# Layer 0 of a two-layer recurrence step in a new order: weight look-ahead, first merges, query products, first key copies

## The chip, the cores and the metric

The kernel runs on one core of a Trainium2 chip. The metric is the time of one execution on the device, in microseconds (us). Three runs of the kernel before gave 788.27, 791.18 and 792.0 us (median 791.18); the execution that was profiled took 789.21 us, of which 787.4 us are the span of the trace.

The engines have short names in the profile: PE is TensorE (matmuls; PEld its weight loads), DVE is VectorE, ACT is ScalarE, POOL is GpSimd, SP is SyncE, which here only issues DMAs. ACT issues DMAs as well. Each engine runs its own instructions strictly in the order in which they stand, and waits at an instruction until the semaphores that it names have come.

## What is computed

One inference step of a two-layer backbone on 128 context tokens and 512 latent tokens (640 tokens, five tiles of 128), width 1024. Layer 0 has two groups of heads, HGRN2 (4 heads, keys of 128) and GLA (4 heads, keys of 64); layer 1 is a retention layer and is not touched here. Each layer is

```python
h = rms_norm(x) * (1 + scale) + shift        # shift, scale, gate = SiLU(cond) @ ada_w + ada_b
p = h @ w_in                                 # queries, keys, values, gates, forget gates
S_t = diag(g_t) S_{t-1} + k_t v_t^T          # one scan per direction, per head
o_t = S_t^T q_t                              # both directions are added
out = (group_rms_norm(o) * silu(gate)) @ w_out
x = x + gate * out
```

In layer 0 the decay g_t differs for every key channel, so that a score between two tokens carries the product of all decays between them.

## The kernel before, in words

Every projection is done in three matmuls, (high, high), (high, low) and (low, high), on operands that were split into a rounded part and a remainder. Weights come in 168 blocks of 128x512: SP loads `raw` (L171, five buffers), ACT rounds it into `wh` (L180), DVE makes the remainder `wl` (L182); `weights(i, look)` issues blocks up to `look` ahead of the one that is used. The activations of layer 0 are split in the same way into `h0h` (ACT, L489) and `h0l` (DVE, L490).

The first stage, from about 20 to 60 us, is the projection `pbv` of the GLA values, in eight steps k. Beside step k the modulation of the activations for step k + 1 is finished (`padv`, `ab`, `xnt`, then `h0h` and `h0l`), and the modulation sums `pada` for step k + 2 run on PE.

Then layer 0 goes through six rows: two GLA rows (two heads each) and four HGRN rows (one head each). A row first projects its queries, keys or forget gates (`pf`, evacuated into `q`, `K` and the decays `T`, which the code calls `g1`). HGRN rows compute K and T from the gates (L817, L819), and `ks`, the sum of both directions' keys (L821). `prepare` multiplies the queries by the decays, once for each direction, into `Q` (L654, L655). The generator `row` then does the scores `px` in a pyramid of seven levels h = 1 ... 64: level h takes a copy `km` of keys in pairs of blocks (`kmix`, ACT, L685), 20 or 40 small matmuls per head on PE, and a masked copy into `A` (L712); then `merge(h)` multiplies half of K (L693) and half of Q (L695) by the decays of their block, and multiplies decays of neighbouring blocks into the table of the next level (L697). After the seventh level K is transposed on PE (`pkt`), copied to `kt` by ACT (L723), multiplied with the values (`pkv`, on PE), and the chunk states `S` are updated on DVE (`states`, L403 and L406: six updates). The outputs are `po<-v,A` and then `po<-S,Q`.

The order on PE is written out by hand: `run` issues the projection of the next row and, whenever a model clock says so, one step of a row (`add_bg`, `step`). The order on the other engines is made by a scheduler, which places an instruction by its priority (as a rule the place at which it was issued) and by when it believes that its inputs are ready. So the steps of two successive rows mix: the projection of row h + 1 runs on PE between the levels of row h, and K, T, ks, Q, the first `km` and the first merge of row h + 1 are issued close to where row h has its `kt`, its states and its outputs.

Of the kernel before, what the change touches and what calls it, by code (L numbers as in the profile page):

```python
# [17 lines left out]
T = 640  # L18
KC = 8
# [9 lines left out]
LOOK = 5  # L29
# [12 lines left out]
def hybrid_kernel(  # L42
# [357 lines left out]
    def states(kv, s, decay, st, out):  # L400

        for n in range(3):
            V.scalar_tensor_tensor(s[:, 0, n + 1, :], s[:, 0, n, :], decay(0, n + 1),  # L403
                                   kv[0][:, 128 * (n + 1):128 * (n + 2)], op0=MUL, op1=ADD)
            m = 3 - n
            V.scalar_tensor_tensor(s[:, 1, m - 1, :], s[:, 1, m, :], decay(1, m + 1),  # L406
                                   kv[1][:, 128 * m:128 * (m + 1)], op0=MUL, op1=ADD)
        for d in range(2):
            S.copy(st[:, d, :], kv[d][:, 0:128])
        ACTQ.dma_start(out, st)  # L410

    def kv_products(heads, kt, vcol):
# [127 lines left out]
    for k in range(KC):  # L540
        wh, wl = weights(ids_bv[k], 1 if k < 6 else LOOK)
        if k + 3 < KC:
            chunks[k + 3] = ada_first(k + 3)
        if k == 5:
            gkw = tokt("gkw")[:, 0:512].rearrange("p (d n) -> p d n", d=2)
            G.memset(gkw, 0.0)
            for gg in range(4):
                for d in range(2):
                    ACTQ.dma_start(gkw[32 * gg + 16 * d:32 * gg + 16 * d + 16, d, :], gla_gk_w[0, d])
            wbl = tokt("wbl")[:, 0:256].rearrange("p (k n) -> p k n", k=KC)  # L550
            ACTQ.dma_start(wbl, w0.rearrange("(k p) n -> p k n", p=128)[:, :, C_BL:C_BL + 32])
        for t in range(NT):
            g, o = group_of(t)
            three(pv[t], wh[:, 0, :], wl[:, 0, :], act[g][0][:, k, o:o + 128], act[g][1][:, k, o:o + 128],
                  k == 0, k == KC - 1, swap=True)
            if k + 1 < KC and t == 0:
                for _ in fin:
                    pass
                first_h(k + 1, 0)
                first_h(k + 1, 1)  # L560
            if k + 2 < KC and t == 1:
                fin = ada_first_mm(k + 2, chunks[k + 2])
                next(fin)
# [86 lines left out]


    def prepare(Q, q, g1):

        G.tensor_tensor(Q[:, 0, :], q, g1[:, 0, :], op=MUL)  # L654
        G.tensor_tensor(Q[:, 1, :], q, g1[:, 1, :], op=MUL)  # L655

    def row(q, g1, K, Q, diag, heads, vcol, ycol, s0, out, y_t, gn):
# [41 lines left out]

        km = kmix(1)  # L700
        kmat, dscale = diag
# [3 lines left out]
        for n, h in enumerate(LEVELS):  # L705
            xs = scores(km, qmix(h))
            merge(h)
            if h < 64:
# [10 lines left out]
        for d, tiles in enumerate((FWD_TILES, BWD_TILES)):  # L719
            p = ps("pkt")  # L720
            for i, t in enumerate(tiles):
                transpose(p[:, 128 * i:128 * i + 128], K[:, d, 128 * t:128 * t + 128])
            S.copy(kt[:, d], p.rearrange("p (t n) -> p t n", t=4))  # L723
        yield D_KT
        kv = kv_products(heads, kt, vcol)
        st = rows.tile([128, 2, 128], F32, tag="st", name="st")
        t128 = g[0]
        states(kv, s, lambda d, t: t128[:, d, t:t + 1], st, out)
        yield D_KV
# [42 lines left out]
    for r in range(2):  # L772
        K, Q, q, g1 = gla[r]

        def use_bq(g, p, q=q):
            off, n = GROUPS[g]
            S.activation(q[:, off:off + n], p[:, :n], AF.Copy, scale=0.125)

        def use_bk(g, p, K=K):
            off, n = GROUPS[g]  # L780
            V.tensor_copy(K[:, 0, off:off + n], p[:, :n])
            S.copy(K[:, 1, off:off + n], p[:, :n])

# [13 lines left out]
    for h in range(4):  # L797
# [22 lines left out]
        ks = t25("ks")  # L820
        G.tensor_tensor(ks, K[:, 0, :], K[:, 1, :], op=ADD)  # L821
        prepare(Q, q, g1)
# [243 lines left out]
```

## Time and profile before

| | |
|---|---|
| median of three runs | 791.18 us |
| the profiled execution | 789.21 us, its span 787.4 us |
| TensorE | 751.2 us busy, 95% of the span |
| VectorE, ScalarE, GpSimd busy | 456.5, 334.7, 90.5 us |
| granted clock, mean over the span | 0.996 of full speed |

The time of a busy TensorE can't be shortened by an order of other engines; what an order can change is the time in which TensorE stands still, and the time in which its clock is low. In a timeline row the bracket at the end tells how long the engine stood still before the instruction, and which instruction of which engine it waited for last. A merged row (x20) stands for a run of like instructions, and its duration for all of them together.

### The profile page before, as it was taken

The numbers are of one execution on the slowest core, as the hardware profiler recorded it, in microseconds if no ns is written. First come the engines' busy times: TensorE is split into PE (matmuls) and PEld (weight loads), VectorE is DVE, ScalarE is ACT, GpSimd is POOL, SyncE is SP. The second block draws the span as 40 slices with busy tenths as digits, with TensorE's granted clock in tenths as the row PEclk, the third lists the DMA queues.
The fourth block names the chain that finished last, engine by engine and source line by source line (L and its number), as shares of the span: only waits on it lengthen the run. The fifth ranks groups of instructions, "written<-read, shape, count | busy, mean of one in ns | idle before, by whom it ended". The sixth has DMA issues, their size and how long they took to land.

```text
span 787.4 us, 15421 instructions
## 1 busy us (share of the span) xinstructions
PE 751.2 (95%) x6116; PEld 658.6 (84%) x6116; DVE 456.5 (58%) x886; ACT 334.7 (43%) x757; POOL 90.5 (11%) x121
## 2 busy tenths in 40 slices
PE   4989889999989999999999999999999999999996
PEld 3668878799989898788888888999999998888885
DVE  4874993844886858563557650346454546336543
ACT  6448734444635353343436450433332432335322
POOL 2000301012130314000001000001121111000101
PEclk9999999999999999999999999999999999999999
DMA  8983440464333331238235520434333332534003
GB/s 286 336 255 111 154 132 25 139 205 125 111 124 119 109 109 50 47 107 261 94 108 174 201 83 25 137 103 102 95 80 113 86 111 81 190 111 133 29 13 134
DMA packets 104775, 98.61 MB, mean 125 GB/s; under 512 B 7660, under 2 KB 80896, under 8 KB 104704
## 3 DMA queue, kind: packets, MB, share of 16 engines
q1 hardware_dynamic: 83520, 82.15, 33.5%
q10 hardware_dynamic: 21184, 15.49, 7.4%
q8 instruction: 48, 0.79, 0.4%
q14 instruction: 23, 0.19, 0.1%
HBM read 86.31 MB, written 8.16 MB: 120 GB/s over the span
## 4 chain that ended last, share of the span: by engine, by line
PE 81%; DVE 10%; issue 4%; DMA 2%; ACT 2%; POOL 1%; ACTq 0%; POOLq 0%; DVEq 0%; SPq 0%
PE pt L85 34%; PE pf L85 24%; PE po L85 6%; PE px L85 5%; PE pkv L85 3%; PE pbv L85 3%; PE pada L85 2%; DVE K L693 2%; DVE wl L182 1%; PE pyt L89 1%; DMA raw<-in_w_in_even_dram 1%; PE pkt L89 1%; DVE Q L695 1%; DVE T L697 1%; DVE A L712 1%
## 5 line engine op out<-in xcount | busy, mean ns | idle before, releaser
L182 DVE TENSOR_TENSOR wl<-raw,wh 128x512 fp32r<-128x512 f32 x168 | 115.5, 704 | 103.1 <-ACT wh L180 98.5
L180 ACT CAST wh<-raw 128x512 fp32r<-128x512 f32 x168 | 103.0, 621 | 90.3 <-PE pf L85 43.0
L85 PE MATMUL pf<-h0h,wh 128*128 128x384 f32 (+1 forms) x256 | 63.2, 328 | 0.0
L85 PE MATMUL pf<-h1h,wh 128*128 128x384 f32 (+1 forms) x256 | 60.3, 317 | 0.0
L85 PE MATMUL pf<-h0l,wh 128*128 128x384 f32 (+1 forms) x256 | 58.4, 309 | 0.0
L85 PE MATMUL pf<-h1l,wh 128*128 128x384 f32 (+1 forms) x256 | 58.3, 309 | 0.0
L85 PE MATMUL pf<-h1h,wl 128*128 128x384 f32 (+1 forms) x256 | 58.3, 309 | 0.0
L85 PE MATMUL pf<-h0h,wl 128*128 128x384 f32 (+1 forms) x256 | 58.3, 309 | 0.0
L685 ACT COPY km<-K 128x640 f32<-128x640 f32 x42 | 32.8, 782 | 52.3 <-DVE K L693 36.7
L333 DVE SCALAR_TENSOR_TENSOR y<-po,rr,gn 128x128 f32<-128x128 f32 x80 | 24.4, 346 | 52.8 <-POOL rr L158 52.8
L85 PE MATMUL pt<-wh,h1h 128*128 128x512 f32 x160 | 53.9, 402 | 0.0
L85 PE MATMUL pt<-wh,h1l 128*128 128x512 f32 x160 | 52.1, 390 | 0.0
L85 PE MATMUL pt<-wl,h1h 128*128 128x512 f32 x160 | 52.0, 390 | 0.0
L156 POOL TENSOR_SCALAR rv<-ss 128x3 f32<-128x3 f32 (+1 forms) x32 | 9.6, 300 | 350.5 <-ACT junk L325 350.0
L695 DVE TENSOR_TENSOR Q<-Q,T 128x640 f32<-128x640 f32 x42 | 38.1, 908 | 14.7 <-PE px L85 14.6
L325 ACT ACTIVATE junk<-po 128x128 f32<-128x128 f32 x80 | 22.3, 279 | 51.8 <-PE po L85 33.8
L693 DVE TENSOR_TENSOR K<-K,T 128x640 f32<-128x640 f32 x42 | 39.8, 948 | 7.2 <-ACT km L685 5.3
L85 PE MATMUL pt<-wh,h0h 128*128 128x512 f32 x120 | 43.5, 428 | 0.0
L85 PEld LDWEIGHTS pf<-h0h,wh 128*128 128x128 f32 x256 | 39.0, 189 | 4.6 <-issue 2.2
L85 PEld LDWEIGHTS px<-Q,km 64*64 64x64 f32 (+1 forms) x1120 | 29.5, 136 | 14.4 <-issue 8.6
L85 PE MATMUL px<-Q,km 64*64 64x64 f32 (+1 forms) x1120 | 35.2, 229 | 4.7 <-DVE Q L695 3.6
L85 PE MATMUL pt<-wh,h0l 128*128 128x512 f32 x120 | 39.7, 396 | 0.0
(218 smaller groups left out, 1594.8 us busy)
## 6 DMA issues: line engine op xcount, KB each, us to landing
raw<-in_w_in_even_dram SPq DMA_DIRECT2D x64, 256.0 KB, 2.9
araw<-in_ada_w_dram SPq DMA_DIRECT2D x64, 256.0 KB, 4.3
raw<-in_w_in_odd_dram SPq DMA_DIRECT2D x64, 256.0 KB, 3.0
ada<-in_ada_w_dram SPq DMA_DIRECT2D x16, 512.0 KB, 5.8
raw<-in_w_out_even_dram SPq DMA_DIRECT2D x24, 256.0 KB, 3.0
rot<-qk ACTq DMA_DIRECT2D x32, 128.0 KB, 3.4
raw<-in_w_out_odd_dram SPq DMA_DIRECT2D x16, 256.0 KB, 3.0
x<-xr SPq DMA_DIRECT2D x5, 512.0 KB, 2.8
```

The lines of the kernel that those rows point to most:

```text
L85: PE.matmul(out, lhsT, rhs, **kw)
L89: PE.transpose(out, in_, ident[0:in_.shape[0], 0:in_.shape[0]])
L156: G.tensor_scalar(v[:, :n], ssum, 1.0 / count, EPS, op0=MUL, op1=ADD)
L180: S.copy(wh, raw)
L182: V.tensor_tensor(wl, raw, wh.bitcast(F32), op=SUB)
L325: S.activation(junk, p[:, 128 * i:128 * i + 128], AF.Square, accum_out=ss[:, j:j + 1])
L333: V.scalar_tensor_tensor(dst, p[:, 128 * i:128 * i + 128], r[:, j:j + 1], dst if have else gn[:, col:col + 128], op0=MUL, op1=MUL)
L685: S.copy(km.rearrange("p (n b h) -> p n b h", b=2, h=h), ap(kf, 0, ([2 * h, T // (2 * h)], [T + h, 2], [1, h])))
L693: V.tensor_tensor(keys, keys, ap(th, 1, ([nn - 1, 2], [2, nb], [0, h])), op=MUL)
L695: V.tensor_tensor(queries, queries, ap(th, 0, ([nn + 1, 2], [2, nb], [0, h])), op=MUL)
L697: V.tensor_tensor(t2, ap(th, 0, ([nn, 2], [2, nb])), ap(th, 1, ([nn, 2], [2, nb])), op=MUL)
L712: V.copy_predicated(A[:, :, 0:64], mask[:, n, :].unsqueeze(1).to_broadcast([128, NT, 64]), x)
```

## The change

Five edits, all in layer 0. The instructions of PE and their order stay the same, row for row.

1. Look-ahead: in the first stage the blocks beyond the next are issued at step k = 7 instead of k = 6. Beside it the small gate weights `gkw` are loaded by two DMAs and spread to the other 96 partitions by three copies on POOL, where eight DMAs on ACT's queue loaded every part.
2. `behind("kt")`: the first `km` of a row is issued behind the `kt` copies of the row before it.
3. `behind("state")`: the first merge of a row (all three multiplications) is issued behind the last state update of the row before it.
4. `prepare` is one multiplication over 1280 columns on DVE instead of two over 640 on POOL, and `ks` moves from POOL to DVE.
5. The copies out of `pf` into `q` and `K` of the GLA rows are issued with high priority.

```diff
@@ states @@
-            V.scalar_tensor_tensor(s[:, 1, m - 1, :], s[:, 1, m, :], decay(1, m + 1),
-                                   kv[1][:, 128 * m:128 * (m + 1)], op0=MUL, op1=ADD)
+            end = V.scalar_tensor_tensor(s[:, 1, m - 1, :], s[:, 1, m, :], decay(1, m + 1),
+                                         kv[1][:, 128 * m:128 * (m + 1)], op0=MUL, op1=ADD)
...
+        return end
@@ first stage @@
-        wh, wl = weights(ids_bv[k], 1 if k < 6 else LOOK)
+        wh, wl = weights(ids_bv[k], 1 if k < KC - 1 else LOOK)
...
-            for gg in range(4):
-                for d in range(2):
-                    ACTQ.dma_start(gkw[32 * gg + 16 * d:32 * gg + 16 * d + 16, d, :], gla_gk_w[0, d])
+            for d in range(2):
+                ACTQ.dma_start(gkw[16 * d:16 * d + 16, d, :], gla_gk_w[0, d])
+            for gg in range(1, 4):
+                G.tensor_copy(gkw[32 * gg:32 * gg + 32], gkw[0:32])
@@ rows @@
+    last = {}
+    def behind(what):
+        return tc.issue_after(last[what].ins) if what in last else ExitStack()
...
-        G.tensor_tensor(Q[:, 0, :], q, g1[:, 0, :], op=MUL)
-        G.tensor_tensor(Q[:, 1, :], q, g1[:, 1, :], op=MUL)
+        V.tensor_tensor(Q, q.unsqueeze(1).to_broadcast([128, 2, T]), g1, op=MUL)
...
-        km = kmix(1)
+        with behind("kt"):
+            km = kmix(1)
...
-            merge(h)
+            with behind("state" if h == 1 else None):
+                merge(h)
...
-            S.copy(kt[:, d], p.rearrange("p (t n) -> p t n", t=4))
+            last["kt"] = S.copy(kt[:, d], p.rearrange("p (t n) -> p t n", t=4))
...
-        states(kv, s, lambda d, t: t128[:, d, t:t + 1], st, out)
+        last["state"] = states(kv, s, lambda d, t: t128[:, d, t:t + 1], st, out)
...
-            S.activation(q[:, off:off + n], p[:, :n], AF.Copy, scale=0.125)
+            with tc.high_priority():
+                S.activation(q[:, off:off + n], p[:, :n], AF.Copy, scale=0.125)
...
-            V.tensor_copy(K[:, 0, off:off + n], p[:, :n])
-            S.copy(K[:, 1, off:off + n], p[:, :n])
+            with tc.high_priority():
+                V.tensor_copy(K[:, 0, off:off + n], p[:, :n])
+                S.copy(K[:, 1, off:off + n], p[:, :n])
...
-        G.tensor_tensor(ks, K[:, 0, :], K[:, 1, :], op=ADD)
+        V.tensor_tensor(ks, K[:, 0, :], K[:, 1, :], op=ADD)
```

Three places show what the scheduler makes of it. The first is ACT in the first stage, from the `h0h` casts of step 5 to those of step 7 (`arow` copies the sums of a modulation step). Before:

```order
L257 COPY arow<-pada 128x128
L180 CAST wh<-raw 128x512
L549 DMA gkw<-in_gla_gk_w_dram 16x256 x3
L180 CAST wh<-raw 128x512 x3
L489 CAST h0h_111<-xnt_109 128x256
L489 CAST h0h_113<-xnt_109 128x384
L257 COPY arow<-pada 128x128
L180 CAST wh<-raw 128x512 x4
L489 CAST h0h_111<-xnt_109 128x256
L489 CAST h0h_113<-xnt_109 128x384
L180 CAST wh<-raw 128x512 x2
```

Now:

```order
L257 COPY arow<-pada 128x128
L180 CAST wh<-raw 128x512 x5
L257 COPY arow<-pada 128x128
L180 CAST wh<-raw 128x512
L490 CAST h0h_111<-xnt_109 128x256
L490 CAST h0h_113<-xnt_109 128x384
L180 CAST wh<-raw 128x512 x2
L490 CAST h0h_111<-xnt_109 128x256
L490 CAST h0h_113<-xnt_109 128x384
L180 CAST wh<-raw 128x512 x2
```

The casts of step 7 (the last two `h0h`) have two weight casts ahead of them where they had four, those of step 6 have six where they had four; the `arow` of step 7 stands behind five of these six.

The second is ACT between the second and the third HGRN row. Before:

```order
L685 COPY km<-K 128x640
L715 COPY A<-px 64x5x64
L716 COPY A<-px 64x5x64
L685 COPY km<-K 128x640
L180 CAST wh<-raw 128x512
L723 COPY kt<-pkt 128x512 x2
L409 COPY st<-pkv 128x128 x2
L410 DMA out_dram<-st 128x2x128
```

Now:

```order
L724 COPY A<-px 64x5x64
L725 COPY A<-px 64x5x64
L180 CAST wh<-raw 128x512
L732 COPY kt<-pkt 128x512 x2
L692 COPY km<-K 128x640
L409 COPY st<-pkv 128x128 x2
L410 DMA out_dram<-st 128x2x128
L692 COPY km<-K 128x640
```

Both `km` copies of the next row stood ahead of the old row's `kt`; now both stand behind it, the second one also behind the copies `st` of the states.

The third is DVE at the same kind of boundary, between the first two HGRN rows (T with a number is a decay table; K, T_25xx belong to the next row, Q with 5x64 and S to the old one). Before:

```order
L817 TENSOR_SCALAR K<-T_2528,nclb,clb 128x1280
L819 TENSOR_SCALAR T_2528<-T_2528,clb,lbv 128x1280
L695 TENSOR_TENSOR Q<-Q,T_2805 128x2x5x64
L693 TENSOR_TENSOR K<-K,T_2528 128x2x320
L697 TENSOR_TENSOR T_3061<-T_2528 128x640
L693 TENSOR_TENSOR K<-K,T_3061 128x2x160x2
L697 TENSOR_TENSOR T_3113<-T_3061 128x320
L182 TENSOR_TENSOR wl<-raw,wh 128x512
...
L403 SCALAR_TENSOR_TENSOR S<-S,T_2878,pkv 128x128 x3
```

Now:

```order
L828 TENSOR_SCALAR K<-T_2522,nclb,clb 128x1280
L830 TENSOR_SCALAR T_2522<-T_2522,clb,lbv 128x1280
L832 TENSOR_TENSOR ks<-K 128x640
L662 TENSOR_TENSOR Q<-q,T_2522 128x1280
L702 TENSOR_TENSOR Q<-Q,T_2799 128x2x5x64
L182 TENSOR_TENSOR wl<-raw,wh 128x512
L403 SCALAR_TENSOR_TENSOR S<-S,T_2871,pkv 128x128 x3
L406 SCALAR_TENSOR_TENSOR S<-S,T_2871,pkv 128x128 x3
L700 TENSOR_TENSOR K<-K,T_2522 128x2x320
L704 TENSOR_TENSOR T_3054<-T_2522 128x640
L704 TENSOR_TENSOR T_3106<-T_3054 128x320
L700 TENSOR_TENSOR K<-K,T_3054 128x2x160x2
```

The first two merges of the next row's keys and its decay tables moved from ahead of the state updates S to behind them; `ks` and the product into Q are new on DVE and stand ahead of the old row's last query merge.

## Rows read from the trace of the kernel before

**Rows 1.** The page, part 1: busy us of each engine, share of the span, instructions

```profile
PE 751.2 (95%) x6116; PEld 658.6 (84%) x6116; DVE 456.5 (58%) x886; ACT 334.7 (43%) x757; POOL 90.5 (11%) x121
```

**Rows 2.** The timeline of PE: start, us, line, tile, count [idle before <-releaser]

```profile
56.31 0.50 PE L85 MATMUL pbv<-wh,h0h 128*128 128x512 f32 x1 [2.07 <-ACT h0h L489]
...
92.73 0.46 PE L85 MATMUL px<-q,K 64*64 64x64 f32 x16 [1.22 <-DVE K L781]
...
94.18 1.05 PE L85 MATMUL px<-Q,km 64*64 64x64 f32 x40 [0.99 <-ACT km L685]
...
100.46 0.83 PE L85 MATMUL px<-Q,km 64*64 64x64 f32 x40 [2.27 <-DVE Q L695]
...
104.43 0.81 PE L85 MATMUL px<-Q,km 64*64 64x64 f32 x40 [0.30 <-DVE Q L695]
...
226.22 1.03 PE L89 MATMUL pkt<-ident,K 128*128 128x128 f32 x8
...
230.38 2.05 PE L85 MATMUL pkv<-v,kt 128*128 128x128 f32 x16 [2.23 <-ACT kt L723]
...
235.03 1.50 PE L85 MATMUL po<-S,Q 128*128 128x128 f32 x12
...
270.02 2.05 PE L85 MATMUL pkv<-v,kt 128*128 128x128 f32 x16 [1.79 <-ACT kt L723]
...
314.31 0.49 PE L85 MATMUL po<-S,Q 128*128 128x128 f32 x2 [0.78 <-DVE S L403]
...
316.33 1.40 PE L85 MATMUL po<-S,Q 128*128 128x128 f32 x10 [1.53 <-DVE S L406]
```

**Rows 3.** The timeline of ACT, 53 to 57 us

```profile
54.47 0.62 ACT L180 CAST wh<-raw 128x512 fp32r<-128x512 f32 x1 [2.39 <-DMA raw<-in_w_in_even_dram]
...
55.85 0.81 ACT L489 CAST h0h<-xnt 128x256 fp32r<-128x256 f32 x2
```

**Rows 4.** The timeline of DVE, first GLA row, 81 to 100 us

```profile
81.27 1.49 DVE L757 TENSOR_TENSOR T<-T,Q 128x1280 f32<-128x1280 f32 x1
...
84.14 4.04 DVE L182 TENSOR_TENSOR wl<-raw,wh 128x512 fp32r<-128x512 f32 x2
...
95.44 0.68 DVE L182 TENSOR_TENSOR wl<-raw,wh 128x512 fp32r<-128x512 f32 x1
...
96.04 2.18 DVE L693 TENSOR_TENSOR K<-K,T 128x640 f32<-128x640 f32 x1
...
98.55 1.77 DVE L695 TENSOR_TENSOR Q<-Q,T 128x640 f32<-128x640 f32 x1
```

**Rows 5.** The timeline of ACT, first GLA row

```profile
80.89 0.74 ACT L777 ACTIVATE q<-pf 128x384 f32<-128x384 f32 x2
```

**Rows 6.** The timeline of ACT between the first two HGRN rows

```profile
228.41 0.79 ACT L685 COPY km<-K 128x640 f32<-128x640 f32 x1 [3.41 <-DVE K L693]
...
229.74 1.07 ACT L723 COPY kt<-pkt 128x512 f32<-128x512 f32 x2
```

**Rows 7.** The timeline of DVE between the first two HGRN rows

```profile
222.23 0.95 DVE L817 TENSOR_SCALAR K<-T,nclb,clb 128x1280 f32<-128x1280 f32 x1
...
226.20 2.17 DVE L693 TENSOR_TENSOR K<-K,T 128x640 f32<-128x640 f32 x1
...
230.56 0.83 DVE L693 TENSOR_TENSOR K<-K,T 128x640 f32<-128x640 f32 x1
...
233.27 1.11 DVE L403 SCALAR_TENSOR_TENSOR S<-S,T,pkv 128x128 f32<-128x128 f32 x3
```

**Rows 8.** The timeline of POOL, two places

```profile
24.60 0.52 POOL L546 MEMSET gkw<- 128x512 f32 x1 [7.85 <-PE pada L85]
...
225.56 2.13 POOL L654 TENSOR_TENSOR Q<-q,T 128x640 f32<-128x640 f32 x1
```

**Rows 9.** The timeline of DVE between the last two HGRN rows

```profile
309.78 3.33 DVE L697 TENSOR_TENSOR T<-T 128x320 f32<-128x320 f32 x2
```

**Rows 10.** Stretches: PE, PEld, DVE, ACT, POOL busy, granted clock, DMA share, GB/s

```profile
317.00:321.00 4.00, 4.00 (x18) 3.42 (x17) 0.81 (x3) 1.12 (x7) 1.05 (x2) 0.57 0.32 76
```

## The prediction

> **What bounds the kernel now.** I read the page's first part, then the waits of TensorE, then around each long wait the timelines of the engine that ended it. TensorE is busy 751.2 of 787.4 us [rows 1], and the order of its instructions does not change, so a gain can come only from its idle time and from its clock. The reader is to see in its timeline that layer 0 has a dozen waits [rows 2], and that they are of four kinds: one in the first stage (2.07), a cluster in the first GLA row (1.22, 0.99, 2.27 and three short ones, the longest 0.30), one at `pkv` behind each of the first two HGRN rows (2.23, 1.79), and a pair at the last one (0.78, 1.53). One more of 0.71 in the second GLA row stays, because the rows around it stand as before. [...]
>
> **First stage (edit 1).** TensorE waits at 56.31 for the `h0h` cast of step 7, which starts at 55.85; the weight casts ahead of it in ACT's order wait for their raw blocks, the one at 54.47 for 2.39 us [rows 2, 3]. The block whose load ends this wait now stands elsewhere: two casts are ahead of step 7, of blocks that are loaded earlier. The two casts and the remainder on VectorE leave perhaps 0.3 us of the 2.07. In exchange step 6 has six weight casts ahead of it, and the last needs a buffer that VectorE frees only after the remainder of the block five places earlier. Nothing in the trace times this load in its new place: if it lands as late as the one in rows 3, the old wait reappears one step earlier and the edit wins nothing; if it lands when it is wanted, nothing is lost. I take 0.2 us, nearer to the second, since ACT no longer issues six of eight `gkw` DMAs between its casts. Edit 1 gives 2.07 - 0.3 - 0.2, about 1.6 us.
>
> The three new copies on GpSimd lie beside VectorE's work of the same steps. Each costs between 0.52 (the memset of 128x512, write only) and 2.13 us (a product with two inputs, 128x640) [rows 8], three 1.6 to 6.4; I take 2, near the memset, because a copy has one input. Their reader stands behind the whole stage, so on the path they cost nothing themselves. But while GpSimd works, an update of K takes 2.17 us on VectorE, without it 0.83 [rows 7]; if the copies do to the remainders and `h0l` what GpSimd's products do to K, VectorE gets 0.83/2.17 of its work done beside them. At 2 us of copies it falls back by 1.2 us, in a stage where it was not last; at 6.4 us by 4, and then all of the 1.6 is gone. [...]
>
> **First GLA row (edits 4 and 5).** The copy of K that TensorE awaits at 92.73 stands in VectorE's order behind the gates of the second row; with priority it comes ahead of them, and the first `km` with it: 1.22 + 0.99 = 2.2 us go. What is late next is the second level. It needs the first merge of Q, which ends VectorE's unbroken queue. In that queue, before, GpSimd's products stretched two remainders to 4.04 where one alone takes 0.68, K to 2.18 and Q to 1.77 where 0.83 is normal [rows 4, 7]: 2.7 + 1.35 + 0.94 = 5.0 us that go. Added are two products over 1280 columns, at the 1.49 of the nearest row (two inputs, same columns) [rows 4], 3.0 us, since the one of the second row is ahead of the merge too; the copies of q, which now come in ACT ahead of half of the logarithms, 0.74 [rows 5]; and some 0.5 of waiting for ACT, less one masked copy of 0.5. VectorE arrives 5.0 - 3.0 - 0.74 = 1.3 us earlier, and the second level starts near 99.2 instead of 100.46 [rows 2]. So of the 2.2 only 1.3 stay: the wait of 2.27 grows to about 3.2. Behind it the decay tables of the second row have left the queue; I count 0.4 of the three short waits. Together 1.7 us. The product is bounded by 1.49 from a row without collision and by 2 x 2.13, what GpSimd took; at the far end the second level is 5.5 us later, and the row loses 4.
>
> **HGRN rows (edits 2, 3 and 4).** Here the mechanism is plain in ACT. `pkt` is done at 227.2 [rows 2]; `kt` is copied at 229.74 only, because `km` of the next row stands ahead and waits 3.41 us for the merge of K on VectorE, itself slow beside GpSimd [rows 6, 7]. Now `kt` stands behind one weight cast that was issued already. It starts at 227.2, takes 1.07, and TensorE, which has projection work until 228.15, finds it ready: at most 0.1 us of each wait is left, 2.1 + 1.7 = 3.8 us gone. The postponed `km` and merge have time: the next row's levels come on TensorE only behind the outputs, which start at 235.03 [rows 2].
>
> What is late next is `po<-S,Q`, for it needs the six state updates. Before, they began at 233.27 behind the next row's merge and tables [rows 7]. Now VectorE's order from 222.23 is K and T (2 x 0.95), `ks` (0.83), the product (1.49), the last merge of Q (0.83) and one remainder (0.68): free at 228. The products `pkv` run from 228.2 for 2.05 us; the updates follow them half way through, 2 x 1.11, and end near 231.5. TensorE wants them, by its distance in rows 2 (235.03 - 232.43 = 2.6 us after `pkv`), at 232.8. That leaves 1.3 us of slack. At the last boundary, VectorE's tables were stretched to 3.33 us [rows 9] in front of the updates; tables and merges now stand behind them, and GpSimd is silent. Of 0.78 + 1.53 I leave 0.2: 2.1 us. Without the pair the clock has no reason to fall there: 1.7 us more.
>
> **Sum.** 1.6 + 1.7 + 3.8 + 2.1 + 1.7 = 10.9 us. Against the profiled execution's own 789.21 that is 778.3. The median of the runs lies 2.0 higher; the mean of all four executions is 790.2, and from that the forecast is 779.3 us.
>
> **Rivals.** (a) The clock falls in the first GLA row. The idle time of some 3.2 us before the second level is longer than any of rows 2, none of which but the last pair brought the clock down. If it falls there as it did behind that pair, 1.7 us are lost again: 781.0. For it: the pair together was only 2.3 us. Against it: 2.27 us at this very place brought nothing down. [...]
>
> (b) The first stage gains nothing, because the wait moves to step 6 or the copies on GpSimd hold VectorE up: 779.3 + 1.6 = 780.9, and with a further 1 us at step 7, 782.
>
> (c) The change doesn't do what it says at the HGRN rows: the weight cast that stands ahead of `kt` waits for its block or for a free buffer as long as `km` did, and the outputs wait for the states. Then only 1.6 + 1.7 remain of the sum, with some of the last pair: 786. Against it: between the end of `km` at 229.20 and `kt` at 229.74 [rows 6] there was room for the cast alone, so it waited for nothing.
>
> (d) Slower than before. VectorE keeps its 2.17 us per 640 columns with GpSimd silent (then the slow rows were not GpSimd's doing): the product costs 4.3 and the sum 2.2 us. What decides is the slack in front of the updates: product and sum may take 2.3 us as forecast, 1.3 of slack, and 1.3 more in which VectorE is free before the products `pkv` are half done. From 4.9 us in a row on, the outputs wait. At 6.5 us they wait 1.6 in each of three rows, the second level of the GLA row comes 2 x 2.8 = 5.6 later and misses the relief of 5.0, and the clock may fall at each of the four places: 779.3 + 4.8 + 5.6 + 5.0 + 6.8 = 801.5. Against it: the same update of K takes 0.83 at 230.56, as soon as GpSimd is done (225.56 + 2.13, and the second product of the pair behind it) [rows 7, 8].
>
> **How the numbers follow.** The forecast has 0.58, with an own range of 776.5 to 782; (a) 0.21, (b) 0.11, (c) 0.06, (d) 0.04. The range of 774.5 to 786 takes in the forecast, (a), (b), the bounds of the unknown load and copies, and the edge of (c). [...] 0.5% is 4.0 us, about what a measurement of this kernel can tell from no change; faster than 787.2 are the forecast, (a), (b) and most of (c): 0.91. Within 0.5%: 0.05. Slower: 0.04.
>
> **What the profile of the changed kernel would show.** Right: no wait over 0.3 us at `pkv` of the HGRN rows and at `po<-S,Q`; full clock from 310 to 320 us; an update of K or T at 0.83 wherever it stands; one product of about 1.5 us per row on VectorE; GpSimd idle in the rows but for norms; one wait of about 3 us before the second level of the first GLA row. Wrong: a wait at step 6 of the first stage; K or `ks` at 2 us without GpSimd; a state update that starts more than 1.5 us after `pkv`; a new wait for `km` at a second level of an HGRN row.

## The result, and the profile after

The changed kernel takes 778.36 us (median of four runs, 777.39 to 778.88) against 789.72 (788.24 to 792.0); the ratio is 0.9851, 95% interval 0.9828 to 0.9875. The profiled execution took 778.65 us, its span 776.9, that is 10.5 us less than the 787.4 of before.

Part 1 of the page, busy us of each engine, share of the span and instructions:

```profile
PE 749.7 (97%) x6116; PEld 658.9 (85%) x6116; DVE 450.4 (58%) x896; ACT 335.6 (43%) x757; POOL 57.5 (7%) x108
```

TensorE does the same work [rows 1] with less waiting; GpSimd has lost 33 us. Since PE's order is the same row for row, the gain can be laid out by stage, from the starts of the same matmuls in both timelines:

| from ... to | before | after | gained |
|---|---|---|---|
| span's start ... first `pbv` | 20.92 | 20.47 | 0.45 |
| ... `plow` (first stage) | 39.29 | 39.23 | 0.06 |
| ... second level of the first GLA row | 40.25 | 38.74 | 1.51 |
| ... its fourth level | 7.90 | 8.86 | -0.96 |
| ... its `pkv` | 17.29 | 16.90 | 0.39 |
| ... `pkv` of the second GLA row | 39.53 | 39.61 | -0.08 |
| ... `pkv` of the first HGRN row | 65.20 | 62.80 | 2.40 |
| ... of the second | 39.64 | 37.58 | 2.06 |
| ... of the third | 39.52 | 39.26 | 0.26 |
| ... of the fourth | 42.13 | 37.75 | 4.38 |

The sum is 10.47. Nearly nine tenths of it, 9.1 us, lie in the last four stages, those of the HGRN rows. The timeline of PE shows it (start, us, line, tile, count [idle before <-releaser]):

```profile
51.89 0.49 PE L85 MATMUL pbv<-wh,h0h 128*128 128x512 f32 x1 [1.63 <-ACT h0h L490]
52.78 0.50 PE L85 MATMUL pbv<-wh,h0l 128*128 128x512 f32 x1 [0.40 <-DVE h0l L491]
...
90.28 0.81 PE L85 MATMUL px<-q,K 64*64 64x64 f32 x40
...
98.44 0.83 PE L85 MATMUL px<-Q,km 64*64 64x64 f32 x40 [3.58 <-ACT km L692]
...
226.61 1.95 PE L85 MATMUL pkv<-v,kt 128*128 128x128 f32 x16
...
231.15 1.50 PE L85 MATMUL po<-S,Q 128*128 128x128 f32 x12
...
264.19 1.95 PE L85 MATMUL pkv<-v,kt 128*128 128x128 f32 x16
...
307.28 1.50 PE L85 MATMUL po<-S,Q 128*128 128x128 f32 x12
```

Of the waits in [rows 2] those at `pkv` and `po<-S,Q` are gone without rest. The first stage has its 2.07 us still, as 1.63 + 0.40, one step earlier. The waits of 1.22 and 0.99 in the first GLA row are gone, and the one of 2.27 before the second level has become 3.58. Behind it the clock fell, to 0.66 from 99 to 104 us. At the boundary of the last two HGRN rows it no longer does, against 0.57 in [rows 10]: the same outputs now start at 307.28, and from there to 321 the clock is at 1.00 (stretch: us, PE, PEld, DVE, ACT, POOL busy, granted clock, DMA share, GB/s):

```profile
99.00:104.00 5.00, 5.00 (x65) 4.74 (x59) 4.21 (x9) 2.16 (x4) 0.00 (x0) 0.66 0.01 3
308.00:313.00 5.00, 5.00 (x47) 4.20 (x48) 3.19 (x11) 3.06 (x12) 1.82 (x4) 1.00 1.04 215
317.00:321.00 4.00, 4.00 (x45) 3.16 (x46) 2.57 (x5) 1.45 (x2) 0.00 (x0) 1.00 0.00 0
```

Between the first two HGRN rows, the timeline of ACT and then that of DVE, against [rows 6, 7]:

```profile
224.75 0.62 ACT L180 CAST wh<-raw 128x512 fp32r<-128x512 f32 x1 [1.67 <-PE pf L85]
225.48 1.07 ACT L732 COPY kt<-pkt 128x512 f32<-128x512 f32 x2
226.44 1.02 ACT L692 COPY km<-K 128x640 f32<-128x640 f32 x1
```

```profile
222.70 0.82 DVE L832 TENSOR_TENSOR ks<-K 128x640 f32<-128x640 f32 x1
223.44 1.48 DVE L662 TENSOR_TENSOR Q<-q,T 128x1280 f32<-128x1280 f32 x1
224.84 0.82 DVE L702 TENSOR_TENSOR Q<-Q,T 128x640 f32<-128x640 f32 x1
...
227.70 1.11 DVE L403 SCALAR_TENSOR_TENSOR S<-S,T,pkv 128x128 f32<-128x128 f32 x3 [1.44 <-PE pkv L85]
228.73 1.11 DVE L406 SCALAR_TENSOR_TENSOR S<-S,T,pkv 128x128 f32<-128x128 f32 x3
229.75 0.82 DVE L700 TENSOR_TENSOR K<-K,T 128x640 f32<-128x640 f32 x1
```

`kt` starts as soon as `pkt` (224.85 to 225.88) has its first half; VectorE is idle for 1.44 us before the updates S, which end at 229.84, 1.31 us before `po<-S,Q` asks for them. Every update of K, Q or T over 640 columns now takes 0.80 to 0.85, where [rows 7] had 2.17.

In the first GLA row the timeline of DVE, and the `km` copy of ACT that PE awaits:

```profile
91.21 0.82 DVE L704 TENSOR_TENSOR T<-T 128x640 f32<-128x640 f32 x1
...
92.55 0.49 DVE L704 TENSOR_TENSOR T<-T 128x320 f32<-128x320 f32 x1
...
93.55 1.24 DVE L704 TENSOR_TENSOR T<-T 128x160 f32<-128x160 f32 x5
...
95.34 1.48 DVE L662 TENSOR_TENSOR Q<-q,T 128x1280 f32<-128x1280 f32 x1
96.74 0.82 DVE L700 TENSOR_TENSOR K<-K,T 128x640 f32<-128x640 f32 x1
```

```profile
97.60 0.79 ACT L692 COPY km<-K 128x640 f32<-128x640 f32 x1 [5.15 <-DVE K L700]
```

The first merge of K could start at about 91, when the scores of the diagonal (`px<-q,K`) have read K. Seven decay tables, three remainders and the second row's product stand ahead of it.

In the first stage, ACT and then DVE and POOL:

```profile
45.63 1.90 ACT L180 CAST wh<-raw 128x512 fp32r<-128x512 f32 x3 [1.24 <-DMA raw<-in_w_in_even_dram]
48.38 1.30 ACT L180 CAST wh<-raw 128x512 fp32r<-128x512 f32 x2 [0.85 <-DMA raw<-in_w_in_even_dram]
...
50.47 0.62 ACT L180 CAST wh<-raw 128x512 fp32r<-128x512 f32 x1 [0.63 <-DMA raw<-in_w_in_even_dram]
51.43 0.90 ACT L490 CAST h0h<-xnt 128x256 fp32r<-128x256 f32 x2 [0.35 <-DVE xnt L487]
```

```profile
46.28 2.72 DVE L182 TENSOR_TENSOR wl<-raw,wh 128x512 fp32r<-128x512 f32 x3 [1.46 <-ACT wh L180]
```

Six casts stand ahead of step 6's `h0h`, and ACT waits three times for their raw blocks, 2.7 us in all. The last 0.35 us before `h0h` is a wait for VectorE's `xnt`, which stands behind the remainders of the same blocks.

### The profile page after: what moved, and what is told of

Same layout as the page of the kernel before. It is cut to its first block, busy times and chain, and to the rows that moved or that the text cites. A ratio compares the mean times of both kernels' runs of the same rounds, so it can differ in the third digit from the quotient of the medians.

```text
span 776.9 us, 15404 instructions
## 1 busy us (share of the span) xinstructions
PE 749.7 (97%) x6116; PEld 658.9 (85%) x6116; DVE 450.4 (58%) x896; ACT 335.6 (43%) x757; POOL 57.5 (7%) x108
## 4 chain that ended last, share of the span: by engine, by line
PE 86%; DVE 5%; issue 3%; DMA 3%; ACT 2%; POOL 1%; ACTq 0%; POOLq 0%; SPq 0%; DVEq 0%
PE pt L85 37%; PE pf L85 26%; PE px L85 6%; PE po L85 6%; PE pkv L85 3%; PE pada L85 2%; DMA raw<-in_w_in_even_dram 2%; PE pbv L85 1%; PE pkt L89 1%; PE pyt L89 1%; PE pxt L89 1%; PE pz L85 1%; DVE wl L182 1%; DVE qk L927 0%; DVE qk L925 0%
## 5 line engine op out<-in xcount | busy, mean ns | idle before, releaser
L692 ACT COPY km<-K 128x640 f32<-128x640 f32 x42 | 32.9, 784 | 39.8 <-DVE K L700 23.4
L702 DVE TENSOR_TENSOR Q<-Q,T 128x640 f32<-128x640 f32 x42 | 34.5, 820 | 16.7 <-PE px L85 16.4
L85 PEld LDWEIGHTS pf<-h0h,wl 128*128 128x128 f32 x256 | 39.6, 191 | 0.0
L85 PEld LDWEIGHTS pf<-h0l,wh 128*128 128x128 f32 x256 | 39.6, 190 | 0.0
```

The lines of the kernel that those rows point to most:

```text
L85: PE.matmul(out, lhsT, rhs, **kw)
L692: S.copy(km.rearrange("p (n b h) -> p n b h", b=2, h=h), ap(kf, 0, ([2 * h, T // (2 * h)], [T + h, 2], [1, h])))
L702: V.tensor_tensor(queries, queries, ap(th, 0, ([nn + 1, 2], [2, nb], [0, h])), op=MUL)
```

## The experiments

Each kernel is built from the changed one unless it says otherwise. Times are medians of four to six runs, ratios are against the kernel before on the same chip.

**Look-ahead from step 6 again (edit 1 taken back).**

```diff
-        wh, wl = weights(ids_bv[k], 1 if k < KC - 1 else LOOK)
+        wh, wl = weights(ids_bv[k], 1 if k < 6 else LOOK)
...
-            for d in range(2):
-                ACTQ.dma_start(gkw[16 * d:16 * d + 16, d, :], gla_gk_w[0, d])
-            for gg in range(1, 4):
-                G.tensor_copy(gkw[32 * gg:32 * gg + 32], gkw[0:32])
+            for gg in range(4):
+                for d in range(2):
+                    ACTQ.dma_start(gkw[32 * gg + 16 * d:32 * gg + 16 * d + 16, d, :], gla_gk_w[0, d])
```

> The changed kernel (778.4 us) with edit 1 taken back: look-ahead from k = 6 again, eight gkw DMAs, no copies on GpSimd. Theory A (edit 1 only moved the wait of about 2.0 us from step 7 to step 6): the wait of about 2 us stands at step 7 again, and the time stays at 778.4, within 0.5 us. Rival B (the prediction's count: edit 1 is worth 1.6): 780.0. Rival C (the copies on GpSimd hold VectorE up and cost what the look-ahead wins): no wait over 1 us at either step would be the sign that both are separate, time 777.

778.19 us, ratio 0.9852 (0.9826 to 0.9877): no measurable difference from the changed kernel, as theory A had it. The wait, 1.68 us, stands at step 7 again.

**The changed kernel once more**, to see whether the wait at step 6 belongs to the order.

> The changed kernel once more, for a second trace of its first stage. If the wait of 2.03 us at step 6 belongs to the order, it stands there again and the stage takes 39.2 us; if it hangs on when the blocks land, the stage takes 37.6 us as in the runs without priority and without the two orders, with a wait under 0.5. All else as before: 777 to 779.

778.03 us, 0.9849 (0.9825 to 0.9872). Step 6 waits 1.86 + 0.38 us in this trace. But five of the other kernels (products on GpSimd again, no order edit, no priority, the first merge ahead, the product late) have the same instructions in this stage, and there the waits at step 6 are between 0.38 and 0.53 us together. In those five ACT waits for raw blocks ahead of step 6's `h0h` for 0 to 1.5 us in all, in the two traces with the long wait for 2.7 and 3.0.

From the first `pbv` to `plow` the traces give, with the look-ahead from step 6 (before and four others), 38.8 to 40.8 us, median 39.8; from step 7 (seven traces), 37.6 to 41.5, median 37.7. So it is neither of the two answers: the order makes the wait possible, and when the raw blocks land, which differs between these traces, decides how long it is.

The copies on GpSimd alone don't make it: with the product late VectorE's remainders are as slow beside them (1.10, 1.09 and 1.02 us, here 1.10, 1.09 and 0.99), ACT waits for no block, and step 6 waits 0.39. The stage times hold the clock too. In the three longest (41.5, 40.8 and 40.7) it fell behind the wait, to 0.79, 0.88 and 0.79 from 52 to 60 us, and with the product late (38.9) it had fallen at the stage's start, to 0.79 from 20 to 28 us.

**Products and `ks` on GpSimd again (edit 4 taken back).**

```diff
-        V.tensor_tensor(Q, q.unsqueeze(1).to_broadcast([128, 2, T]), g1, op=MUL)
+        G.tensor_tensor(Q[:, 0, :], q, g1[:, 0, :], op=MUL)
+        G.tensor_tensor(Q[:, 1, :], q, g1[:, 1, :], op=MUL)
...
-        V.tensor_tensor(ks, K[:, 0, :], K[:, 1, :], op=ADD)
+        G.tensor_tensor(ks, K[:, 0, :], K[:, 1, :], op=ADD)
```

> The changed kernel (778.4 us) with edit 4 taken back: the two products per row and ks on GpSimd again, all order edits kept. Theory A (VectorE's slow updates, 1.8 to 2.2 us for 640 columns, are GpSimd's collision): these come back in the stretches where GpSimd works, the second level of the first GLA row starts some 1.3 us later, the updates S of the HGRN rows are late by up to 1 us, time 780 to 783. Rival B (there is slack enough, only the order matters): 778.4, within 0.5 us, with the 2.17 us updates still there but waited for by nobody. Rival C (product on VectorE costs more than it saves): below 777.5.

781.14 us, 0.9892 (0.9863 to 0.9922), 2.8 above the changed kernel. The loss is all in the first GLA row: the second level waits 5.21 instead of 3.58, and from `plow` to the row's `pkv` it is 67.15 us against 64.50. In the HGRN rows the four steps between `pkv` are 62.80, 37.58, 39.27, 37.74 as in the table, though VectorE's updates are slow again. So theory A is right for the first GLA row and rival B for the HGRN rows. The timelines of DVE and POOL between the first two HGRN rows show how slow:

```profile
223.40 0.95 DVE L831 TENSOR_SCALAR T<-T,clb,lbv 128x1280 f32<-128x1280 f32 x1
224.26 2.19 DVE L703 TENSOR_TENSOR Q<-Q,T 128x640 f32<-128x640 f32 x1
```

```profile
223.51 2.26 POOL L833 TENSOR_TENSOR ks<-K 128x640 f32<-128x640 f32 x1 [24.39 <-DVE K L829]
```

GpSimd's sum ends at 225.77; VectorE's update, with two inputs, ends 0.68 us later. Before, it was the same: the product ended at 227.69 [rows 8] and K at 228.37 [rows 7]. The TENSOR_SCALAR beside the sum, with one tensor, keeps its 0.95, but it had begun 0.11 us ahead of the sum. For the fourth HGRN row the sum begins first, and the timelines of DVE and then POOL show the reverse, a slow TENSOR_SCALAR and a faster sum:

```profile
298.82 2.00 DVE L831 TENSOR_SCALAR T<-T,clb,lbv 128x1280 f32<-128x1280 f32 x1
```

```profile
298.55 1.59 POOL L833 TENSOR_TENSOR ks<-K 128x640 f32<-128x640 f32 x1 [21.60 <-DVE K L829]
```

**No order edit behind `kt` and the states (edits 2 and 3 taken back).**

```diff
-        with behind("kt"):
-            km = kmix(1)
+        km = kmix(1)
...
-            with behind("state" if h == 1 else None):
-                merge(h)
+            merge(h)
```

> The changed kernel (778.4 us) with edits 2 and 3 taken back: km and the first merge of a row are no longer behind the kt copies and the states of the row before. Theory A (the order of ACT and VectorE is the cause of the waits behind the HGRN rows): waits of about 2 us at pkv behind the first two HGRN rows come back, and some at po<-S,Q of the last one with its clock fall: 784 to 787. Rival B (the waits were made by GpSimd's collision, which stretched the merge of K to 2.17 us, and with the products on VectorE the order alone costs little): waits under 0.8 us at pkv, 779 to 780.5.

777.81 us, 0.9841 (0.9813 to 0.9868): theory A is refuted. No wait at `pkv` or `po<-S,Q`, the four steps are 62.80, 37.58, 39.27, 37.74. ACT, then DVE, at the first boundary:

```profile
225.19 1.07 ACT L730 COPY kt<-pkt 128x512 f32<-128x512 f32 x2
226.15 0.85 ACT L692 COPY km<-K 128x640 f32<-128x640 f32 x1
```

```profile
225.28 0.82 DVE L700 TENSOR_TENSOR K<-K,T 128x640 f32<-128x640 f32 x1
```

Here the second `km` comes behind `kt` without being told to: with `ks` and the product ahead of the merge of K on VectorE, the scheduler places `km` later. That leaves two readings, the changed order or the missing collision.

**The kernel before, with GpSimd nearly silent.** Products and sum stay on GpSimd, but over 32 columns; the rest of the product into Q and of `ks` is left out.

```diff
-        G.tensor_tensor(Q[:, 0, :], q, g1[:, 0, :], op=MUL)
-        G.tensor_tensor(Q[:, 1, :], q, g1[:, 1, :], op=MUL)
+        G.tensor_tensor(Q[:, 0, 0:32], q[:, 0:32], g1[:, 0, 0:32], op=MUL)
+        G.tensor_tensor(Q[:, 1, 0:32], q[:, 0:32], g1[:, 1, 0:32], op=MUL)
...
-        G.tensor_tensor(ks, K[:, 0, :], K[:, 1, :], op=ADD)
+        G.memset(ks, 0.0); G.tensor_tensor(ks[:, 0:32], K[:, 0, 0:32], K[:, 1, 0:32], op=ADD)
```

> The kernel before (790.8 us), with its order on PE, VectorE and ScalarE, but GpSimd silent: the products into Q and the sum ks are made over 32 columns instead of 640 (the rest of Q and ks is left out; ks is cleared by a memset). VectorE has no product to do either. Theory A (the waits behind the HGRN rows are made by GpSimd's collision alone: the last merge of Q and the merge of K at 2.2 us each put km, and so kt, late): with 0.83 each km ends 2.7 us earlier, before pkt is done, and the waits at pkv fall from 2.23 and 1.79 to under 0.2, those at po<-S,Q with the clock fall go too; with the shorter first GLA row 776 to 779. Rival B (the order on ScalarE, km ahead of kt, is what costs): waits of over 0.8 us stay at pkv, 781 to 785.

777.27 us, 0.9839 (0.9813 to 0.9864). The four steps are 62.80, 37.58, 39.27, 37.74 once more. Through layer 0's rows, up to 330 us, the order of ACT and VectorE is that of before, instruction for instruction, but for a copy, a gate and two small tables that change places at the last boundary: `km`, cast, `kt` on ACT, merge and tables ahead of S on VectorE. DVE, then ACT:

```profile
221.59 0.88 DVE L695 TENSOR_TENSOR Q<-Q,T 128x640 f32<-128x640 f32 x1
222.39 0.87 DVE L693 TENSOR_TENSOR K<-K,T 128x640 f32<-128x640 f32 x1
```

```profile
223.30 0.82 ACT L685 COPY km<-K 128x640 f32<-128x640 f32 x1 [0.78 <-DVE K L693]
224.01 0.64 ACT L180 CAST wh<-raw 128x512 fp32r<-128x512 f32 x1
224.67 1.08 ACT L723 COPY kt<-pkt 128x512 f32<-128x512 f32 x2
```

In the kernel before, DVE had there:

```profile
224.08 2.20 DVE L695 TENSOR_TENSOR Q<-Q,T 128x640 f32<-128x640 f32 x1
```

K takes 0.87 instead of 2.17, and the merge of Q ahead of it 0.88 instead of 2.20. Together they are 2.6 us shorter, and the wait for `km` that holds ACT up is shorter by as much, 0.78 instead of 3.41 us [rows 6]. Theory A holds: with the order unchanged, taking the collision away was enough to end the waits.

**The kernel before, with edit 2 alone** (`km` behind `kt`).

> The kernel before (790.8 us) with edit 2 alone: km behind kt, the products and ks on GpSimd as before. Theory A (two queues are held up by GpSimd's collision, ScalarE's and VectorE's; freeing the first hands the wait to the second): the waits at pkv go, but the updates S still stand behind slow merges and tables, and waits of 0.5 to 2 us come at po<-S,Q; time 787 to 790. Rival B (ScalarE's order was all that TensorE waited for): no wait at pkv nor at po<-S,Q of the first two HGRN rows, time 785 to 786.5.

787.75 us, 0.9951 (0.9934 to 0.9969), 3.35 us below the median of before; theory A. No wait at `pkv`, but new ones behind it. DVE at the first boundary, then PE:

```profile
227.49 4.80 DVE L698 TENSOR_TENSOR T<-T 128x640 f32<-128x640 f32 x5
...
233.63 0.72 DVE L403 SCALAR_TENSOR_TENSOR S<-S,T,pkv 128x128 f32<-128x128 f32 x2
```

```profile
235.19 1.38 PE L85 MATMUL po<-S,Q 128*128 128x128 f32 x10 [0.67 <-DVE S L406]
...
273.72 1.38 PE L85 MATMUL po<-S,Q 128*128 128x128 f32 x10 [0.67 <-DVE S L406]
...
313.37 0.49 PE L85 MATMUL po<-S,Q 128*128 128x128 f32 x2 [0.79 <-DVE S L403]
...
315.39 2.03 PE L85 MATMUL po<-S,Q 128*128 128x128 f32 x10 [1.53 <-DVE S L406]
```

Tables that collide with GpSimd, and a merge behind them, hold the updates up until 233.63, and the pair at the last boundary stands unchanged.

**The kernel before, with edit 4 alone.**

> The kernel before (790.8 us) with edit 4 alone: products and ks on VectorE, no order edit, look-ahead and priority as before. Theory A (edit 4 carries the whole gain): pkv to pkv takes 62.8, 37.6, 39.3 and 37.7 us as in the changed kernel, no wait at pkv or po<-S,Q, time within 1 us of the changed kernel's 778.0 to 778.4. Rival B (the order edits cover for each other, and one of them is needed): 0.5 us or more come back at some pkv or po<-S,Q, 779.5 to 783.

780.55 us, 0.9861 (0.9838 to 0.9884). The four steps are 62.80, 37.58, 39.27, 37.74: the waits did not come back, against rival B. The time is 2 us above the changed kernel all the same; in this trace the first stage took 40.79 us, and `plow` to the first `pkv` 64.87 against 64.50. Edit 4 carries the 9.1 us of the HGRN rows, as theory A has it; its time is missed, and in this trace what is left lies ahead of those rows.

**No priority (edit 5 taken back).** The `with tc.high_priority():` around the copies of q and K go.

> The changed kernel (778.4 us) with edit 5 taken back: copies of q and K of the GLA rows without priority. Theory A (the second level of the first GLA row is bound by VectorE's queue, not by the first copies of K): waits of 1 to 2 us for K or km come back at the diagonal and first level, the wait at the second level shrinks by as much, its start stays near 98.4 us; time 778.4 or, since the idle time is then split into shorter pieces and the clock need not fall to half behind it, down to 776.8. Rival B (the prediction's count, where 2.2 us of K and km waits go and the rest is queue): those waits come back in full, 780.6.

777.54 us, 0.985 (0.9821 to 0.9879): theory A. Waits of 0.78 and 0.90 come back, the one at the second level shrinks from 3.58 to 0.87, and `plow` to `pkv` takes 64.31 against 64.50. Edit 5 moved a wait and won nothing that can be measured. The clock, which theory A thought might be spared, fell here too, to 0.88 from 94 to 99 us.

**The first merge ahead.** Tables, and the second row's product, behind the first row's first merge on VectorE.

```diff
-            V.tensor_tensor(queries, queries, ap(th, 0, ([nn + 1, 2], [2, nb], [0, h])), op=MUL)
+            last.setdefault("merge", V.tensor_tensor(queries, queries, ap(th, 0, ([nn + 1, 2], [2, nb], [0, h])), op=MUL))
...
-            V.tensor_tensor(t2, ap(th, 0, ([nn, 2], [2, nb])), ap(th, 1, ([nn, 2], [2, nb])), op=MUL)
+            with behind("merge"): V.tensor_tensor(t2, ap(th, 0, ([nn, 2], [2, nb])), ap(th, 1, ([nn, 2], [2, nb])), op=MUL)
...
-        V.tensor_tensor(Q, q.unsqueeze(1).to_broadcast([128, 2, T]), g1, op=MUL)
+        with behind("merge"): V.tensor_tensor(Q, q.unsqueeze(1).to_broadcast([128, 2, T]), g1, op=MUL)
```

> The changed kernel (778.4 us) with the decay tables of the first GLA row and the query product of the second queued behind the first merge of the first GLA row on VectorE. Theory A (the 3.58 us before the second level are VectorE's queue: five tables, a product and two remainders ahead of the merge of K; and the clock falls because of this wait): the wait falls under 0.5 us, the clock stays at 1.00 from 99 to 104, time 778.4 - 3.3 - 1.0 = 774. Rival B (what is put back is late at the next levels): waits of 0.5 to 1.5 us at the third and fourth level, 775.5 to 777. Rival C (the clock falls there for another reason): 775, with the clock still at 0.6 to 0.7.

775.85 us, 0.9821 (0.9796 to 0.9846): rival B. The 3.58 become 0.25 and the clock stays at 1.00 from 99 to 104 us, but the product now stands between two merges, and waits of 0.81 and 1.03 come at the third and fifth level.

**Casts beyond the first stage behind the last `h0h`**, their remainders behind the last `h0l`.

```diff
-        wh, wl = weights(ids_bv[k], 1 if k < KC - 1 else LOOK)
+        with behind("h" if k == KC - 1 else None), behind("l" if k == KC - 1 else None): wh, wl = weights(ids_bv[k], 1 if k < KC - 1 else LOOK)
```

> The changed kernel (778.4 us) with the weight casts and remainders of the blocks beyond the first stage queued behind the last h0h and h0l. Theory A (casts that wait for their raw blocks stand ahead of h0h on ScalarE, and remainders ahead of ab and xnt on VectorE; how long depends on when the blocks land, which differs from run to run): no wait over 0.2 us at steps 6 and 7, the first stage (first pbv to plow) takes 37.3 us or less instead of 37.6 to 39.2; time 776.5 to 778. Rival B (the postponed casts and remainders delay low and the gates): what is won in the first stage is lost before the first GLA row, 778.4 or up to 780.

778.04 us, 0.9842 (0.9821 to 0.9864). The stage takes 36.61 us, without a wait at steps 6 and 7, the shortest so far; 0.91 us are lost at once, since `low` stands behind seven casts. No gain that can be measured: between A and B.

**The product late.** As with the first merge ahead; the second GLA row's product is issued at that row's start, behind the states of the first.

```diff
-        prepare(Q, q, g1)
+        if r == 0: prepare(Q, q, g1)
...
+        with behind("state"): prepare(Q, q, g1) if diag[1] == 2.0 and "kt" in last else None
```

> The changed kernel with the first merge of the first GLA row ahead of the decay tables (as in the run with that edit, 775.85), and the second GLA row's query product behind the states of the first row instead of between its merges. Theory A (the waits of 0.81 and 1.03 us at the third and fifth level were the product's 1.5 us): both fall under 0.3 us, the product is hidden in VectorE's idle time behind the states, time 774. Rival B (something else in the queue holds the levels, or the second row's first level now waits for its product): 775.5 to 777.

773.31 us (773.15 to 775.06), 0.9776 (0.9755 to 0.9797): theory A, the best of all, 5 us below the changed kernel. PE, and the stretch behind the second level:

```profile
95.79 0.83 PE L85 MATMUL px<-Q,km 64*64 64x64 f32 x40 [0.25 <-DVE Q L702]
...
103.43 0.81 PE L85 MATMUL px<-Q,km 64*64 64x64 f32 x40 [0.16 <-ACT km L692]
```

```profile
99.00:104.00 5.00, 4.79 (x125) 4.07 (x126) 4.96 (x11) 1.45 (x2) 0.00 (x0) 1.00 0.28 80
```

`plow` to `pkv` takes 60.21 us against 64.50.

**Both**: the late product, and the casts behind `h0h`, two of them behind `low`.

> The kernel with the late product, and in the first stage the weight casts and remainders of the blocks beyond it behind the last h0h and h0l, two of them behind low. Theory A: first stage (first pbv to plow) of 36.6 us as with the look-ahead behind h0h, and the wait of 0.91 us for low shrinks, since five casts stand ahead of low instead of seven: 0.9 to 2 us below the kernel with the late product alone, 772 to 773.5. Rival B (the gates come late, since casts stand among them, and the first level of the first GLA row waits for its product): 774 to 775.

775.98 us, 0.9803 (0.9783 to 0.9823), 2.7 worse than the late product alone: worse than rival B had it. The stage takes 36.60 us, but the scheduler now puts the first row's product behind a gate of the second; PE waits 0.73 us for it at the first level and 2.35 at the second:

```profile
97.57 1.34 PE L85 MATMUL px<-Q,km 64*64 64x64 f32 x40 [2.35 <-DVE Q L703]
```

```profile
94.00:99.00 5.00, 2.65 (x50) 2.30 (x48) 5.00 (x10) 0.80 (x1) 0.00 (x0) 0.85 0.85 250
```

## Why the prediction was right, and where it was not

**The time.** 779.3 was said, 778.36 measured; 10.9 us by the sum, 10.5 in the traces. The total is right, but by luck in part: two terms came out 2.3 us short together, those of the HGRN rows 1.5 us above what was said, and 0.45 us ahead of the first `pbv` belongs to no term. The term of 1.7 us for the clock is 4 x 0.43, an estimate from the 4 us at 0.57 in [rows 10], where the changed kernel shows 1.00. The lower end of the range is where all the idle time that the prediction lists and these 1.7 us are won, 2.1 + 5.2 + 4.0 + 2.3 + 1.7, some 15 us.

**First stage, 1.6 us.** It gave 0.06 in the profiled pair. The step that failed is "I take 0.2 us, nearer to the second": the block landed late, and the old wait came back one step earlier, which was the far end of the bound and rival (b). In five of seven traces the estimate would have held. As to the three copies on GpSimd, they took 2.77 us where 2 was taken, and cost the remainders beside them 1.1 us (1.10, 1.09 and 0.99 for 0.68); priced as in the prediction, 2.77 us of copies would have cost 1.7. The times can't tell edit 1 from nothing.

**First GLA row, 1.7 us.** The step that VectorE arrives 1.3 us earlier holds: the second level comes 1.5 us earlier after `plow`, the product takes 1.48, and the wait is 3.58 where 3.2 was said. What failed is that the clock would hold: 0.66 from 99 to 104. That is rival (a). The 0.96 us of the table is a net loss, for the short waits of before, 0.30 and 0.17 us ahead of the third and fourth level, went as well; the low clock itself cost some 1.4 by an estimate from these (0.96 + 0.47), near its price of 1.7. Without it the row would have won 2.4, with it 0.9. That edit 5 was worth 2.2 less what the queue takes back was too kind: no run shows that it is worth anything.

**HGRN rows, 3.8 us, last pair and clock, 2.1 + 1.7 = 3.8.** Measured 2.40 + 2.06 + 0.26, and 4.38. The size is right, somewhat low, and so is the slack before the outputs, 1.3 us said and 1.31 found. What failed is the cause: "Here the mechanism is plain in ACT", with the order as what had to change. The order edits are enough (products back on GpSimd: no wait) but not needed (edits 2 and 3 taken back: no wait), and edit 2 alone only hands the wait on to `po<-S,Q`. One cause lies under both queues, GpSimd's collision: with GpSimd nearly silent, the old order has no wait at `pkv` or `po<-S,Q` at all. The row for this was in the prediction, K at 2.17 and 0.83 [rows 7], and so was the sentence that VectorE gets 0.83/2.17 of its work done; it was priced for the copies and the GLA row, and not carried through to ACT's `km`, which stood behind two merges that were 1.3 us too slow each.

How VectorE and GpSimd collide, the rows show: a two-input update that began beside GpSimd's instruction ended 0.68 us after it, so that most of its own 0.82 us lies behind it (226.45 against 225.77 with the products on GpSimd again, 228.37 against 227.69 before). It goes both ways round: an update beside a sum that had begun took 2.19 for 0.82 of work; the TENSOR_SCALAR, which reads one tensor, kept its 0.95 where it had begun first and the sum took 2.26, and took 2.00 where the sum had begun first and took 1.59. In these pairs the one that began first kept its time, and the one that began second took 0.67 to 1.37 us longer than its shortest, an instruction with one tensor too. So the prediction's share of 0.83/2.17 is no rate that holds for every pair. Nor do the pairs give a rule: at the last boundary of the kernel before, an update of Q kept 0.81 though it began at 305.66, 0.16 us behind GpSimd's product, and the product took 5.66.

**Rivals (c) and (d).** No wait at `kt`'s cast, no slow K without GpSimd; both are refuted. In the chances, 0.91 for faster than 787.2 leaves (c) only 0.01 of its 0.06, where the prediction says most of it.

**What stays open.** Edits 1, 2, 3 and 5 together are worth 2 us by the medians of edit 4 alone and of the changed kernel (780.55, 778.36), and the intervals, some 2 us either way, overlap.

## What to carry to other kernels

When two queues are late at one place, look for the one resource under both before reordering either: moving the work off GpSimd did alone, in the HGRN rows, what two order edits did together. An estimate for a load that no row times is a draw: in such a stage compare several traces, because one can say 0.4 and the next 2.2 us (the waits at step 6). A wait that an edit shortens must be followed to the next row of the same queue: the copies with priority and the product between the merges each only moved it.

## What was not expected of the hardware

- The clock does not follow the length of one wait. In the first GLA row it fell behind a wait of 3.58 to 3.62 us in five of five traces (0.61 to 0.88 in the 5 us from 99 or, where the wait ended later, from 104) and behind one of 5.21 us (0.50 from 99 to 104). But it also fell at two waits of 0.78 and 0.90 us (no priority, 0.88 from 94 to 99), of 0.79 and 0.90 (edit 4 alone, 0.66 from 94 to 99) and of 0.73 and 2.35 (late product and late casts, 0.85 from 94 to 99), and it did not at 0.78 and 0.99 (GpSimd nearly silent, 1.00 from 94 to 109) or at 1.22, 0.99 and 2.27 (before, 1.00 from 94 to 109). In the first stage, behind waits of 1.6 to 2.1 us, it fell to 0.79 to 0.88 (52 to 60 us) in three traces and stayed at 1.00 in four. Each of these falls stands behind idle time of TensorE; these runs don't show what tells the cases apart.
- The collision costs GpSimd time as well. In the kernel before, a product or sum over 640 columns took 1.55 to 1.59 us where it began ahead of VectorE's instruction (95.98, 195.26 and 303.08), and 2.0 to 2.3 behind one; at the last boundary the two products took 5.66 and 1.81. Over 32 columns (GpSimd nearly silent) those between VectorE's updates took 0.76 to 0.95. So 0.5 to 0.6 us of the 2.13 of [rows 8] are the collision's, by an estimate from these times.
- In the HGRN rows TensorE's stages repeat: without waits at `pkv` and `po<-S,Q` the four steps between `pkv` agree within 0.02 us over eleven kernels whose ACT and VectorE orders differ. The first stage varied by 5 us over the same traces (36.6 to 41.5), with the landing of blocks, the clock and the place of the casts.
